# The value products of four attentions: one unit later in TensorE's order, low parts of the probabilities in a second sweep

## The chip, the cores and the metric

The kernel runs on one core of a Trainium2 chip. The metric is the device time of one execution in microseconds (us); the time before is the median of three runs.

## What is computed

Two blocks of a transformer on 512 tokens of width 1024, all in float32. The first block has a latent attention of 8 heads ("mla"), a short convolution, an attention of 4 heads over 256 memory rows ("mem"), gates and an output projection. The second has two causal attentions of 8 heads each, "fox" (with a bias from cumulated forget gates) and "dil" (windows of three dilations, folded into one mask), an output projection, and a layer of product-key experts. What the change touches is in each attention this:

```python
s = einsum('bqhd,bkhd->bhqk', q, k) * scale      # + bias, mask
p = softmax(s, axis=-1)
o = einsum('bhqk,bkhd->bqhd', p, v)
```

The experts come after all attentions, and take the second half of the time.

## The kernel before, in words

*Products in two parts.* TensorE works on rounded float32 (fp32r). Each operand x is split into a high part, hi (ScalarE copies x into the rounded type, L174 or L177 of `split`), and a low part, lo = x - hi (VectorE, L175 or L178). A product is then three matmuls into one PSUM tile, weights hi by data hi, hi by lo, lo by hi: L182, L183 and L184 of `mm`, or L194, L195 and L197 of `mtile`. In the trace these lines are the helper's; the tile tells which product it is: "mm" for scores, projections and gates (4 PSUM tiles), "tp" for transposes (2), "o" for value products (2).

*An attention in units.* `attention` (L321) cuts the work into units: one head h and one block i of 128 queries, so 16 units for mem, and 32 each for mla, fox and dil. nkc(i) is the number of chunks of 128 keys that block i looks at: 2 in mem, 4 in mla, i + 1 in fox and dil. The steps of a unit are: `s` scores (TensorE), `e` softmax without the division (VectorE and ScalarE, L308 to L315), `norm` division (VectorE L341 and L346, or ScalarE L344), `tr` transposes of the probabilities (TensorE, L354), `sp` split of the transposed probabilities from PSUM into a tile PT (ScalarE L174, VectorE L175), and `o` the value product (TensorE) with its evacuation. Two units, i even and odd, share one PT tile of 128 x 2 x 4 x 256 (hi and lo, key chunk, query), and `o` runs once for the pair, after the odd unit: for each key chunk three matmuls, vh by PT hi, vh by PT lo, vl by PT hi, over 256 queries, or over 128 for a chunk that only the odd unit looks at. So an `o` has 6 matmuls in mem, 12 in mla, and 6 or 12 in fox and dil. There are 8 + 16 + 16 + 16 = 56 of them.

*The order that is written.* Step j of `attention` writes out: scores of unit j; division and transposes of j - 1; softmax of j; split of j - 1; value product of j - 2. The attention has n + 2 such steps. Between steps, `merge` puts other tasks ("fills": gate, convolution, projection products) by their costs; mla's 34 steps of cost 2.0 share the fills in proportion, mem's first 14 steps and fox's and dil's first 32 have fills as well. `run` gives each task its weights, 4 loads ahead.

*The order that is run.* The whole program is handed to a scheduler at build time, which lists each engine's instructions: earlier written ones come first, but an instruction whose operands are not there yet, by the scheduler's own model of time, is passed by later ones that are ready. Engines then run their lists in order. SBUF tiles of the kind of PT (`b8`) come from a pool of NB8 = 16 buffers, and a new tile waits until an old one has had its last reader.

Of the kernel before, what the change touches and what calls it, by code (L numbers as in the profile page):

```python
# [25 lines left out]
              n1=8, n2=8, bfor=1, qh=96, kh=96, qhc=1, khc=1)  # L26
# [82 lines left out]
class Kernel:  # L109
# [211 lines left out]
    def attention(self, nh, nkc, scores, probs, v, evac, prep=None, cost=1.5, act=False):  # L321

        nc = self.nc
        units = [(h, i) for h in range(nh) for i in range(4)]
        st = {}

        def s(j):
            h, i = units[j]  # L330
            st["s", j] = self.psum("mm")
            scores(h, i, st["s", j])

        def e(j):
            h, i = units[j]
            st["P", j] = probs(h, i, st.pop(("s", j)))

        def norm(j):
            h, i = units[j]
            P, c = st["P", j]  # L340
            nc.vector.reciprocal(c[:, 3:4], c[:, 2:3])  # L341
            p = P[:, :nkc(i) * 128]
            if act:
                nc.scalar.activation(p, p, AF.Copy, scale=c[:, 3:4])  # L344
            else:
                nc.vector.tensor_scalar(p, p, c[:, 3:4], None, op0=ALU.mult)  # L346

        def tr(j):
            h, i = units[j]
            P, _ = st.pop(("P", j))  # L350
            n = nkc(i)
            tp = self.psum("tp")
            for kc in range(n):
                nc.tensor.transpose(tp[:, kc * 128:(kc + 1) * 128], P[:, kc * 128:(kc + 1) * 128],  # L354
                                    self.cst("ident"))
            st["t", j] = tp

        def sp(j):
            h, i = units[j]
            n = nkc(i)  # L360
            if i % 2 == 0:
                st["PT", h, i // 2] = self.b8(F32R, [128, 2, 4, 256])
            pt = st["PT", h, i // 2]
            q = (i % 2) * 128
            src = st.pop(("t", j))[:, :n * 128].rearrange("p (a b) -> p a b", a=n)
            self.split(pt[:, 0, :n, q:q + 128], pt[:, 1, :n, q:q + 128], src)

        def o(j):
            h, i = units[j]
            if i % 2 == 0:  # L370
                return
            pt = st.pop(("PT", h, i // 2))
            ps = self.psum("o")
            n0, n1 = nkc(i - 1), nkc(i)
            for kc in range(n1):
                c = slice(0, 256) if kc < n0 else slice(128, 256)
                vh, vl = v(h, kc)
                self.mm(ps[:, c], vh, vl, pt[:, 0, kc, c], pt[:, 1, kc, c], kc == 0, kc == n1 - 1)
            evac(h, i // 2, ps)

        tasks = []
        n = len(units)
        for j in range(n + 2):
            def step(j=j):
                if j < n:
                    h, i = units[j]
                    if prep is not None and i == 2 and h + 1 < nh:
                        prep(h + 1)
                    s(j)
                if 0 <= j - 1 < n:  # L390
                    norm(j - 1)
                    tr(j - 1)
                if j < n:
                    e(j)
                if 0 <= j - 1 < n:
                    sp(j - 1)
                if 0 <= j - 2 < n:
                    o(j - 2)
            tasks.append(Task(step, None, cost))
        return tasks  # L400

# [1429 lines left out]
```

## Time and profile before

| | us |
|---|---|
| median of three runs | 2168.97 (2168.51, 2168.97, 2172.50) |
| profiled execution | 2168.01 |
| its span on the core | 2166.3 |
| TensorE busy | 2113.3 |
| VectorE busy | 1652.2 |
| ScalarE busy | 976.5 |

The span is the time from the first to the last instruction of the program on the core. Busy time of TensorE is the union of its matmuls, whose ends are modelled; how fast they follow each other is seen from the differences of their starts. "Idle before" in brackets is the time in which the engine did nothing before an instruction, and behind the arrow stands the instruction whose end released it.

### The profile page before, as it was taken

What the parts mean: (1) busy time and instruction counts of PE and PEld (TensorE: products, weight loads), DVE (VectorE), ACT (ScalarE), POOL (GpSimd) and SP (SyncE); (2) the same over time, 40 slices, a digit from 0 to 9 for tenths busy, and PEclk for the clock granted to TensorE, in tenths of its full rate; (3) what the DMA queues carried; (4) which work ended last, traced back from release to release, by engine and by line L of the source; (5) the groups of instructions that cost most, each with busy time, mean ns of one, the idle gap of its engine ahead of it and who ended that gap; (6) DMA issues with size and microseconds to landing.
All of it is one profiled execution on the core that took longest, in us unless ns stands there. A gap on an engine that the chain in (4) does not pass through costs nothing. (4 is left out here: it accounts for less than half of the span.)

```text
span 2166.3 us, 30072 instructions
## 1 busy us (share of the span) xinstructions
PE 2113.3 (98%) x11091; PEld 1819.0 (84%) x11091; DVE 1652.2 (76%) x3491; ACT 976.5 (45%) x1493; POOL 486.1 (22%) x349
## 2 busy tenths in 40 slices
PE   8999999999999999999999899999999999999998
PEld 6787787888877888789999899999998888888786
DVE  6755565633457778799999999989859878877877
ACT  6454355623334555433344555566644333333332
POOL 0000000011200000100053454645544222222332
PEclk9999999999999999999999999999999999999999
DMA  6122211123323122222498898999999999999994
GB/s 226 57 87 69 88 59 49 59 88 136 93 86 110 47 60 78 62 76 78 157 356 295 296 342 316 348 338 340 343 326 348 331 340 353 331 344 345 325 345 160
DMA packets 159411, 448.86 MB, mean 207 GB/s; under 512 B 12952, under 2 KB 62872, under 8 KB 155552
## 3 DMA queue, kind: packets, MB, share of 16 engines
q1 hardware_dynamic: 114768, 265.26, 35.6%
q0 software_dynamic: 44352, 181.42, 22.6%
q8 instruction: 87, 1.43, 0.3%
q14 instruction: 60, 0.49, 0.1%
q10 hardware_dynamic: 144, 0.26, 0.0%
HBM read 397.59 MB, written 49.30 MB: 206 GB/s over the span
## 5 line engine op out<-in xcount | busy, mean ns | idle before, releaser
L174 ACT ACTIVATE whi<-wraw 128x1024 fp32r<-128x1024 f32 x388 | 408.8, 1054 | 685.9 <-PE mm L195 319.7
L175 DVE TENSOR_TENSOR wlo<-wraw,whi 128x1024 fp32r<-128x1024 f32 x388 | 471.1, 1215 | 186.5 <-ACT whi L174 125.6
L194 PE MATMUL mm<-b,whi 128*128 128x384 f32 (+1 forms) x1656 | 603.9, 366 | 8.2 <-ACT b L174 5.3
L195 PE MATMUL mm<-b,whi 128*128 128x384 f32 (+1 forms) x1656 | 596.2, 361 | 0.7 <-DVE b L175 0.7
L197 PE MATMUL mm<-b,wlo 128*128 128x384 f32 (+1 forms) x1656 | 369.0, 361 | 2.8 <-DVE wlo L175 2.8
L194 PEld LDWEIGHTS mm<-b,whi 128*128 128x128 f32 x1656 | 311.1, 188 | 39.8 <-ACT b L174 5.8
L195 PEld LDWEIGHTS mm<-b,whi 128*128 128x128 f32 x1656 | 311.2, 188 | 30.4 <-DVE b L175 2.5
L197 PEld LDWEIGHTS mm<-b,wlo 128*128 128x128 f32 x1656 | 297.5, 187 | 32.3 <-DVE wlo L175 3.4
L1662 PE MATMUL mm<-whi,b 128*128 128x512 f32 x1024 | 301.5, 394 | 0.0
L1521 POOL DMA_INDIRECT b<-in_peer_v,eidx x128 | 204.6, 1599 | 322.4 <-PE mm L1662 203.2
L1521 POOL DMA_INDIRECT b<-in_peer_un,eidx x128 | 194.7, 1521 | 256.1 <-PE mm L1662 88.2
L1662 PEld LDWEIGHTS mm<-whi,b 128*128 128x128 f32 x1024 | 192.3, 188 | 45.3
L1556 DVE SCALAR_TENSOR_TENSOR b<-b,gg,b 128x1024 f32<-128x1024 f32 x128 | 163.5, 1277 | 3.5 <-DMA b<-in_peer_v,eidx 3.4
L1550 DVE CUSTOM_DVE_ANT_0 b<-b,b 128x1024 f32<-128x1024 f32 x128 | 155.1, 1215 | 8.4 <-DMA b<-in_peer_un,eidx 8.4
L1662 PE MATMUL mm<-wlo,b 128*128 128x512 f32 x512 | 161.2, 394 | 0.0
L174 ACT ACTIVATE b<-b 128x384 fp32r<-128x384 f32 (+2 forms) x160 | 86.5, 546 | 164.2 <-DVE b L1630 125.1
L1662 PE MATMUL o<-whi,b 128*128 128x512 f32 x512 | 160.5, 394 | 0.0
L182 PE MATMUL mm<-b,whi 128*128 128x512 f32 x320 | 127.8, 399 | 2.9 <-ACT b L315 2.0
L184 PE MATMUL mm<-b,wlo 128*128 128x512 f32 x320 | 127.8, 399 | 0.0
L183 PE MATMUL mm<-b,whi 128*128 128x512 f32 x320 | 127.4, 398 | 0.0
L1662 PEld LDWEIGHTS mm<-wlo,b 128*128 128x128 f32 x512 | 96.2, 188 | 22.9
L1662 PEld LDWEIGHTS o<-whi,b 128*128 128x128 f32 x512 | 96.2, 188 | 22.6
(301 smaller groups left out, 3008.4 us busy)
## 6 DMA issues: line engine op xcount, KB each, us to landing
wraw<-in_peer_u SPq DMA_DIRECT2D x128, 512.0 KB, 6.2
wraw<-in_peer_v SPq DMA_DIRECT2D x128, 512.0 KB, 6.6
wraw<-in_w_in_ft SPq DMA_DIRECT2D x57, 512.0 KB, 3.4
gdram<-b POOLq DMA_DIRECT2D x24, 1024.0 KB, 9.3
b<-gdram SPq DMA_DIRECT2D x32, 768.0 KB, 12.9
hdram<-b POOLq DMA_DIRECT2D x28, 768.0 KB, 7.4
b<-hdram SPq DMA_DIRECT2D x28, 768.0 KB, 9.1
wraw<-in_w_out SPq DMA_DIRECT2D x16, 512.0 KB, 3.5
```

The costliest lines, as they stand in the source:

```text
L174: nc.scalar.activation(hi, x, AF.Copy)
L175: nc.vector.tensor_tensor(lo, x, hi.bitcast(F32), op=ALU.subtract)
L182: t.matmul(out, lhsT=wh, rhs=xh, start=start, stop=False)
L183: t.matmul(out, lhsT=wh, rhs=xl, start=False, stop=False)
L184: self.last = t.matmul(out, lhsT=wl, rhs=xh, start=False, stop=stop)
L194: t.matmul(ps[:M], lhsT=wh[:, k], rhs=xh(k), start=k == 0, stop=False)
L195: t.matmul(ps[:M], lhsT=wh[:, k], rhs=xl(k), start=False, stop=False)
L197: self.last = t.matmul(ps[:M], lhsT=wl[:, k], rhs=xh(k), start=False, stop=k == nk - 1)
L1521: d = nc.gpsimd.indirect_dma_start(out=t, out_offset=None, in_=a["peer_un" if kind == "u" else "peer_v"], in_offset=bass.IndirectOffsetOnA ...
L1550: nc.vector.tensor_tensor_reduce(t, t, st["xy"][:, 0], 1.0, 0.0, ALU.mult, ALU.add, st["hg"][:, s:s + 1])
L1556: nc.vector.scalar_tensor_tensor(st["xy"][:, 1], t, st["gg0"][:, s:s + 1], st["xy"][:, 1], op0=ALU.mult, op1=ALU.add)
L1662: K.last = nc.tensor.matmul(acc[2 * tt + j], lhsT=w[:, c], rhs=d, start=m == 0 and e == 0, stop=m == 127 and e == 2)
```

## The change

It touches `o` and the loop over steps in `attention`, and so all four attentions. In `o`, the three matmuls of a key chunk are no longer written together: a first sweep over the chunks writes vh by PT hi and vl by PT hi, a second sweep vh by PT lo. And step j writes the value product of unit j - 3 instead of j - 2; the attention has n + 3 steps. The steps before it are unchanged.

```diff
             n0, n1 = nkc(i - 1), nkc(i)
+
+            cols = lambda kc: slice(0, 256) if kc < n0 else slice(128, 256)
             for kc in range(n1):
-                c = slice(0, 256) if kc < n0 else slice(128, 256)
                 vh, vl = v(h, kc)
-                self.mm(ps[:, c], vh, vl, pt[:, 0, kc, c], pt[:, 1, kc, c], kc == 0, kc == n1 - 1)
+                nc.tensor.matmul(ps[:, cols(kc)], lhsT=vh, rhs=pt[:, 0, kc, cols(kc)], start=kc == 0, stop=False)
+                nc.tensor.matmul(ps[:, cols(kc)], lhsT=vl, rhs=pt[:, 0, kc, cols(kc)], start=False, stop=False)
+            for kc in range(n1):
+                self.last = nc.tensor.matmul(ps[:, cols(kc)], lhsT=v(h, kc)[0], rhs=pt[:, 1, kc, cols(kc)],
+                                             start=False, stop=kc == n1 - 1)
             evac(h, i // 2, ps)
 
         tasks = []
         n = len(units)
-        for j in range(n + 2):
+        LAG = 3
+        for j in range(n + LAG):
...
-                if 0 <= j - 2 < n:
-                    o(j - 2)
+                if 0 <= j - LAG < n:
+                    o(j - LAG)
```

## Rows read from the trace of the kernel before

**Rows 1.** The page: span, TensorE's busy time, and its granted clock by slices.

```profile
span 2166.3 us, 30072 instructions
...
PE 2113.3 (98%) x11091; PEld 1819.0 (84%) x11091; DVE 1652.2 (76%) x3491; ACT 976.5 (45%) x1493; POOL 486.1 (22%) x349
...
PEclk9999999999999999999999999999999999999999
```

**Rows 2.** Busy time of the engines in the four attention stretches.

```profile
core 0: us, PE busy (x) PEld busy (x) DVE busy (x) ACT busy (x) POOL busy (x), PEclk, DMA share, GB/s
130.00:185.00 55.00, 51.80 (x278) 43.40 (x278) 29.67 (x94) 32.41 (x79) 0.00 (x0) 1.00 0.18 60
265.00:440.00 175.00, 170.89 (x902) 141.55 (x901) 104.86 (x203) 100.16 (x177) 5.18 (x4) 1.00 0.17 58
680.00:785.00 105.00, 100.75 (x592) 84.60 (x592) 81.07 (x263) 57.40 (x144) 0.00 (x0) 1.00 0.18 56
785.00:880.00 95.00, 90.47 (x512) 76.28 (x510) 74.55 (x223) 49.82 (x120) 0.00 (x0) 1.00 0.17 56
sum 430.00, PE 413.91 PEld 345.84 DVE 290.15 ACT 239.78 POOL 5.18; mean PE 103.48 PEld 86.46 DVE 72.54 ACT 59.95 POOL 1.30
```

**Rows 3.** TensorE's waits, whole span: waiting, released by: total us, times, longest.

```profile
PE mm L464 <- ACT whi L177: 6.5, 2, 5.4
PE tp L1485 <- ACT b L1492: 6.2, 2, 5.5
...
PE mm L182 <- ACT b L315: 4.3, 10, 0.8
PE o L183 <- DVE b L175: 3.6, 7, 1.0
...
PE mm L182 <- DVE t L308: 2.1, 2, 1.2
PE o L182 <- ACT b L174: 1.4, 3, 0.7
...
PE tp L354 <- DVE b L178: 0.7, 1, 0.7
```

**Rows 4.** TensorE in order of time, fox: start, duration, instruction, idle before.

```profile
734.33 0.36 PE L182 MATMUL o<-b,b 128*128 128x256 f32 x1
734.62 0.50 PE L182 MATMUL mm<-b,b 128*128 128x128 f32 x2
736.14 0.38 PE L183 MATMUL o<-b,b 128*128 128x256 f32 x1 [1.02 <-DVE b L175]
736.37 0.28 PE L184 MATMUL o<-b,b 128*128 128x256 f32 x1
736.48 0.28 PE L182 MATMUL o<-b,b 128*128 128x256 f32 x1
736.60 0.28 PE L183 MATMUL o<-b,b 128*128 128x256 f32 x1
```

**Rows 5.** VectorE in the same stretch.

```profile
735.40 0.69 DVE L175 TENSOR_TENSOR b<-tp,b 128x512 fp32r<-128x512 f32 x1
```

**Rows 6.** TensorE in order of time, mem: two lone first matmuls.

```profile
147.41 0.29 PE L182 MATMUL o<-b,b 128*128 128x256 f32 x1
148.27 0.50 PE L182 MATMUL mm<-b,whi 128*128 128x512 f32 x1 [0.57 <-ACT b L315]
...
166.38 0.36 PE L182 MATMUL o<-b,b 128*128 128x256 f32 x1
167.31 0.39 PE L182 MATMUL mm<-b,b 128*128 128x256 f32 x1 [0.56 <-ACT b L315]
```

**Rows 7.** TensorE in order of time, end of dil.

```profile
867.46 0.28 PE L182 MATMUL o<-b,b 128*128 128x256 f32 x1
...
870.33 0.38 PE L182 MATMUL o<-b,b 128*128 128x256 f32 x1 [0.58 <-ACT b L174]
871.05 0.39 PE L183 MATMUL o<-b,b 128*128 128x256 f32 x1 [0.34 <-DVE b L175]
...
873.29 0.39 PE L182 MATMUL o<-b,b 128*128 128x256 f32 x1 [0.16 <-ACT b L174]
...
875.75 0.38 PE L182 MATMUL o<-b,b 128*128 128x256 f32 x1 [0.69 <-ACT b L174]
876.47 0.39 PE L183 MATMUL o<-b,b 128*128 128x256 f32 x1 [0.34 <-DVE b L175]
```

**Rows 8.** TensorE and, at 777.45, ScalarE in order of time, fox.

```profile
692.48 0.22 PE L182 MATMUL o<-b,b 128*128 128x128 f32 x1
692.53 0.27 PE L183 MATMUL o<-b,b 128*128 128x128 f32 x1
692.64 0.28 PE L184 MATMUL o<-b,b 128*128 128x128 f32 x1
...
776.85 0.28 PE L184 MATMUL o<-b,b 128*128 128x128 f32 x1
...
777.45 0.78 ACT L174 ACTIVATE b<-tp 128x256 fp32r<-128x256 f32 x2
...
777.86 0.38 PE L182 MATMUL o<-b,b 128*128 128x256 f32 x1
779.48 0.39 PE L182 MATMUL mm<-b,b 128*128 128x256 f32 x1 [1.23 <-DVE t L308]
...
784.72 0.27 PE L184 MATMUL o<-b,b 128*128 128x128 f32 x1
```

**Rows 9.** TensorE in order of time, mla.

```profile
333.34 0.39 PE L182 MATMUL o<-b,b 128*128 128x256 f32 x1
334.10 0.50 PE L182 MATMUL mm<-b,whi 128*128 128x512 f32 x1 [0.37 <-ACT b L315]
```

**Rows 10.** Value products by line, whole span; and weight loads of L183, by form.

```profile
L182 PE MATMUL o<-b,b x176: 220/282/388, 147.4 to 877.5; 128*128 128x256 f32 x144, 128*128 128x128 f32 x32
L183 PE MATMUL o<-b,b x176: 273/282/387, 152.8 to 877.6; 128*128 128x256 f32 x144, 128*128 128x128 f32 x32
L184 PE MATMUL o<-b,b x176: 273/281/364, 152.9 to 877.7; 128*128 128x256 f32 x144, 128*128 128x128 f32 x32
...
L183 PEld LDWEIGHTS o<-b,b 128*128 128x128 f32 x176 | 33.3, 189 | 6.8 <-DVE b L175 5.5
```

**Rows 11.** ScalarE's waits, 592 to 880 us.

```profile
ACT b L174 <- PE o L184: 32.2, 21, 3.1
```

## The prediction

> **What bounds the kernel now.** I read the page first: TensorE is busy 98% of the span, and its clock is at the higher of its two levels nearly everywhere [rows 1]. So a gain can only come from time in which TensorE stands still, or from fewer or cheaper matmuls; the change has as many matmuls as before. Then I read the stretches with attention in them [rows 2]: the memory attention (130 to 185 us), the latent attention (265 to 440), fox (680 to 785) and dil (785 to 880). TensorE is busy 413.9 of these 430 us, so 16.1 us of standing still is all that the attentions have. VectorE is busy 77 and 78% in the two causal stretches; it is behind at places, not bound.
>
> Then the waits of TensorE [rows 3]. Four of the groups belong to the attentions: the value products that wait for the low parts of the probabilities (3.6 us in 7 waits) and for the high parts (1.4 us in 3), and score or gate products on L182 that wait for ScalarE's exp to read its PSUM tile (4.3 us in 10) or for VectorE's L308 (2.1 us in 2). The two largest single waits of the page's list, at L464 and L1485, lie outside.
>
> Last the order itself. A value product (tile o) takes its first matmul, then stops: the next one needs the low parts, which VectorE subtracts after ScalarE's copy. In fox [rows 4] the first o matmul starts at 734.33, two score matmuls start behind it, and then TensorE stands still for 1.02 us until VectorE's subtraction, started at 735.40, is through [rows 5]. All 11 remaining o matmuls of that unit waited for this one subtraction, though the four products with the high parts on vh and the four on vl needed nothing but what the first matmul had. Of the 56 value products of the four attentions, 47 have such a lone first matmul, the first at 147.41 and the last at 867.46 [rows 6, 7].
>
> **The change part by part.** *(a) The waits of the value products themselves.* 3.6 + 1.4 = 5.0 us [rows 3]. One unit further back means that a whole unit of TensorE work lies between the split of the probabilities and their use. A unit in fox lasts (784.72 - 692.64) / 30 = 3.07 us, from the last matmul of fox's first value product to that of its sixteenth [rows 8]; the longest wait is 1.0 us [rows 3]. The cover is three times the longest wait, so away from the ends these waits go. At the end of dil nothing else is left to fill [rows 7]: there 0.58, 0.34, 0.16, 0.69 and 0.34 us, 2.1 of the 5.0, are spent. After the change the value product of unit 29 (six matmuls, 0.7 us) moves behind the last transposes, and the last one starts its eight high-part products (8 x 0.12 = 0.94 us, the spacing of [rows 4]) when ScalarE is done. That covers the 0.34 us for the low parts and 0.5 of the 0.69 us. I keep 0.5 us there and take 4.5 us of gain; the bounds are 2.9 us (the tail keeps all) and 5.0.
>
> *(b) Starting up again.* The matmul that ended a wait has its successor 0.23 us later (736.14 to 736.37), a running one 0.12 us later [rows 4]. Ten waits by 0.11 us is 1.1 us; I take 1.0 (bounds 0 and 1.1).
>
> *(c) Stalls right behind a lone o matmul.* TensorE, with nothing else ready in the order that was written out, goes on to a score or gate product whose PSUM tile is not yet free: 0.93 us from start to start at 166.38 and 0.86 at 147.41 [rows 6], 0.76 at 333.34 and three times more at other heads [rows 9], 1.62 at 777.86 [rows 8]. Less the 0.12 us that the matmul takes, the seven sum to 0.93 + 0.86 + 4 x 0.76 + 1.62 - 7 x 0.12 = 5.6 us. A value product whose operands are all there has 6 or 12 matmuls (0.7 or 1.4 us) to put in that place, more than each stall but one. Whether it stands there depends on the order that the scheduler draws up, and some of the products will already have been used up earlier. Bounds 0 and 5.6; the rows show neither end as nearer, I take half, 2.8.
>
> *(d) Lone matmuls.* Most cost nothing: the next instruction starts 0.12 us later. A dozen have it 0.20 us later; 12 x 0.08 = 1.0 us, of which I take 0.5 (bounds 0 and 1.0).
>
> *(e) The second sweep.* Before, vh was used twice in a row and then vl; after, vh, vl, and vh again later. The instruction count is the same: 176 + 176 + 176 matmuls [rows 10]. Each of them has a weight load of its own: the 176 products with low parts have 176 loads of 189 ns, though the matmul before had the same weights [rows 10]. So I put the second sweep at zero. The Trainium skill, "TensorE: Matmul & The Clock Gate", Part 2, says that weights typically stay put and can be loaded once for several matmuls; by that the change would lose 176 reuses. The trace has no such reuse here to lose. In fox and dil the last chunk is 128 columns wide: of its three matmuls the second comes 0.06 us after the first, the third 0.11 us after that [rows 8]. After the change the third stands alone behind a 256-column one; by these two spacings that is at most 32 x 0.05 = 1.6 us either way. I take zero.
>
> *(f) What runs on.* Each attention has one more step at its end. In the latent attention the fills are spread over 35 steps instead of 34, so the end still has cover; fox runs straight into dil; the memory attention's end runs into gate products. Only dil's end is bare, counted in (a). No DMA is added or removed, and VectorE's, ScalarE's and GpSimd's own work is the same; what reads tile o (the evacuations on ScalarE or VectorE) comes with it one unit later in their queues. Nothing is put ahead of SyncE's weight loads but by the shift of the fills.
>
> The sum: 4.5 + 1.0 + 2.8 + 0.5 = 8.8 us. TensorE that doesn't stop at one place comes sooner to the next that waits for the same late engine; VectorE has over a fifth of its time free [rows 2] and can make most of that up, so I give back 0.8 us and take 8.0. The profiled execution took 2168.0 us (span 2166.3 and 1.7 around it), so it would be 2160.0. The median of the three runs is 1.0 us above it: 2161.
>
> **The rivals.** *The wait only moves.* If VectorE's lateness is what counts, TensorE waits as long at the next transpose or score. For it: the score products already wait 2.1 us for L308. Against it: the transposes of L354, which close the chain of the softmax, have one wait of 0.7 us in the whole list [rows 3]. It would leave the time at 2165 to 2171.
>
> *Everything near tile o goes.* All of (a) to (d) at the upper bound is 5.0 + 1.1 + 5.6 + 1.0 = 12.7 us: 2156 on the scale of the median, and with some of the stalls between score products 2152.
>
> *The probability tiles run out (slower).* They come from a pool of 16 buffers, and in fox 14 are taken (normed input 4, residual 2, forget rows 2, values 4, output 2), so two are left. The split of unit 2p+4 has to wait until value product p has read its tile. In fox that split already follows closely: the last o matmul of unit 27 starts at 776.85 and ScalarE's splits at 777.45 [rows 8], a margin of 0.6 us less the matmul's own time, while ScalarE waits for the end of value products for 32.2 us in 21 waits [rows 11]. If the product now comes a unit (3.07 us) later than the transposes of that split, the margin turns into some 1.5 to 2.5 us of delay, and both PSUM tiles for transposes stay full. Sixteen pairs by 1.5 us is 24 us if no projection fills it, 12 us if half is filled; less the 8 us of gain that gives 2173 to 2185, and I take 2179. It decides at one point: whether a ready value product is put ahead of the transposes two units on. In the order as written it is, and nothing that it reads is late any more; that speaks against it.
>
> *The lost reuse of weights*, by the rule named in (e): 176 loads of 0.19 us that were not there before is 33 us, 2202. The rows have the loads already.
>
> **How the numbers follow.** The forecast (2156 to 2164.5, likeliest 2161) has 0.48; everything near tile o goes (2152 to 2156) 0.12; the wait only moves (2165 to 2171) 0.24; the tiles run out 0.14; lost reuse 0.02. A different order may also shift stalls in the later stages, which I count in the width of each. The range that leaves out no more than two in ten goes from 2151 to 2173. What a measurement can tell from no change is about 0.2%, 4.3 us: faster, under 2164.6, 0.60; within, 0.26; slower, 0.14.
>
> **What the profile after would show.** Right: the rows for o matmuls waiting for L174 and L175 are gone but for the last one in dil; value products stand in unbroken runs of 6 or 12; TensorE's idle time in the four stretches falls from 16 us to about 10. Wrong: the same microseconds beside waits of transposes or scores (the wait moved), or ScalarE's splits waiting longer for value products and TensorE's transposes behind them (the tiles ran out). Wrong in the sum: lone first matmuls remain although the operands are there, because the scheduler still breaks the products up.

## The result and the profile after

The changed kernel takes 2154.6 us (median of six runs, 2152.8 to 2155.0) against 2168.7 us (2167.7 to 2172.5): the ratio is 0.9932, with a 95% interval of 0.9922 to 0.9942. That is 14.2 us less; 8 were forecast. It is faster and inside the range, but below the forecast's own bracket (2156 to 2164.5) and where the rival "everything near tile o goes" had put it (2152 to 2156).

The page of after [rows 1]:

```profile
span 2153.2 us, 30081 instructions
...
PE 2107.9 (98%) x11091; PEld 1819.7 (85%) x11091; DVE 1651.9 (77%) x3491; ACT 977.0 (45%) x1493; POOL 467.9 (22%) x349
```

The span fell by 13.1 us. TensorE has the same 11091 matmuls, yet its busy time fell by 5.4 us (2113.3 to 2107.9). So only 7.7 us of the 13.1 were time that the trace shows as standing still; the other 5.4 us had been booked as work. That is where the sum was too small.

The busy times of the four stretches [rows 2], same windows:

```profile
130.00:185.00 55.00, 52.72 (x281) 43.94 (x280) 29.59 (x96) 33.28 (x83) 0.00 (x0) 1.00 0.20 68
265.00:440.00 175.00, 171.16 (x908) 143.06 (x907) 104.16 (x204) 100.22 (x178) 5.17 (x4) 1.00 0.17 58
680.00:785.00 105.00, 103.68 (x620) 87.95 (x619) 87.45 (x274) 59.93 (x149) 0.00 (x0) 1.00 0.18 56
785.00:880.00 95.00, 93.90 (x526) 80.53 (x525) 76.19 (x214) 54.73 (x123) 3.94 (x3) 1.00 0.19 62
```

TensorE stands still for 8.5 us there instead of 16.1, and it is in fox (1.3 for 4.3) and dil (1.1 for 4.5) that it stopped less. In fox 620 matmuls fall into the 105 us, where 592 did. (The last window holds more than dil now, whose last value product starts at 866.8.)

TensorE's waits, whole span [rows 3]:

```profile
PE tp L1491 <- ACT b L1498: 6.3, 3, 4.9
...
PE mm L182 <- ACT b L177: 4.1, 5, 1.6
PE o L379 <- ACT b L174: 2.4, 3, 1.1
PE mm L182 <- ACT b L315: 1.6, 4, 0.8
...
PE mm L182 <- DVE t L308: 0.9, 1, 0.9
```

L379 and L380 are the first sweep (vh, vl by PT hi), L382 the second (vh by PT lo); lines further down are six higher than before, L1485 is L1491. No value product waits for low parts any more (3.6 us in 7 before). Waiting for the high parts went up, from 1.4 to 2.4 us in 3. Score products wait less for L315 (4.3 to 1.6) and L308 (2.1 to 0.9), those on L177 more (4.1).

TensorE in fox, the place of [rows 4] (start, duration, instruction):

```profile
734.41 0.50 PE L354 MATMUL tp<-c_all,b 128*128 128x128 f32 x3
734.67 0.36 PE L379 MATMUL o<-b,b 128*128 128x256 f32 x1
734.87 0.28 PE L380 MATMUL o<-b,b 128*128 128x256 f32 x1
734.99 0.22 PE L379 MATMUL o<-b,b 128*128 128x128 f32 x1
735.05 0.28 PE L380 MATMUL o<-b,b 128*128 128x128 f32 x1
735.16 0.62 PE L354 MATMUL tp<-c_all,b 128*128 128x128 f32 x4
735.54 0.42 PE L382 MATMUL o<-b,b 128*128 128x256 f32 x2
735.80 0.44 PE L182 MATMUL mm<-b,b 128*128 128x128 f32 x2
```

A value product now starts with all its high-part matmuls, transposes of another unit stand between its two sweeps, and no bracket is left.

*Where the 13.1 us went.* I cut both traces at four instructions, into five stretches. From the start to mem's last value product: 193.6 and 193.4 us. From there to fox's first: 497.4 and 496.2 (mla lies in it). From there to dil's last: 186.7 and 177.1. From there to the first product of the experts: 131.3 and 129.0. The rest: 1157.3 and 1157.4. So 9.6 + 2.3 us of it are fox and dil with their tail, and 1.3 us all the rest of the attentions. Below, "C" is the third of these, fox's first to dil's last value product: 186.7 before, 177.1 after. In C TensorE stands still for 7.0 us before and 1.0 after.

### The profile page after: what moved, and what is told of

Read it like the earlier page. It is cut to its first block, busy times and chain, and to the rows that moved or that the text cites. A ratio compares the mean times of both kernels' runs of the same rounds, so it can differ in the third digit from the quotient of the medians.

```text
span 2153.2 us, 30081 instructions
## 1 busy us (share of the span) xinstructions
PE 2107.9 (98%) x11091; PEld 1819.7 (85%) x11091; DVE 1651.9 (77%) x3491; ACT 977.0 (45%) x1493; POOL 467.9 (22%) x349
## 4 chain that ended last, share of the span: by engine, by line
PE 90%; DVE 8%; ACT 1%; issue 0%; DMA 0%; SPq 0%; DVEq 0%; ACTq 0%
PE mm L1668 17%; PE mm L194 14%; PE mm L197 14%; PE mm L195 13%; PE o L1668 8%; PE mm L182 6%; PE mm L183 5%; PE mm L184 5%; PE tp L1491 2%; PE tp L354 1%; DVE wlo L175 1%; PE o L379 1%; PE o L380 1%; PE o L382 1%; DVE b L1304 1%; DVE tk L1302 1%
## 5 line engine op out<-in xcount | busy, mean ns | idle before, releaser
L1527 POOL DMA_INDIRECT b<-in_peer_v,eidx x128 | 198.1, 1548 | 334.2 <-PE mm L1668 203.7
L1527 POOL DMA_INDIRECT b<-in_peer_un,eidx x128 | 183.1, 1430 | 255.0 <-PE mm L197 90.0
L183 PE MATMUL mm<-b,whi 128*128 128x512 f32 x320 | 127.4, 398 | 0.0
```

The source lines that it names most:

```text
L183: t.matmul(out, lhsT=wh, rhs=xl, start=False, stop=False)
L1527: d = nc.gpsimd.indirect_dma_start(out=t, out_offset=None, in_=a["peer_un" if kind == "u" else "peer_v"], in_offset=bass.IndirectOffsetOnA ...
```

## What held ScalarE: a loop that the traces don't bear out

[Rows 11] stood in the prediction only as evidence on buffers. They suggest a mechanism of their own, which has to be checked. ScalarE in fox, before (start, duration, instruction, idle before):

```profile
732.96 0.38 ACT L174 ACTIVATE b<-o 64x256 fp32r<-64x256 f32 x1
733.36 0.60 ACT L174 ACTIVATE b<-tp 128x512 fp32r<-128x512 f32 x1
...
737.68 0.38 ACT L174 ACTIVATE b<-o 64x256 fp32r<-64x256 f32 x1 [2.19 <-PE o L184]
738.09 0.39 ACT L174 ACTIVATE b<-tp 128x256 fp32r<-128x256 f32 x1
```

and VectorE in the same place:

```profile
733.08 0.69 DVE L1086 TENSOR_TENSOR b<-mm,b 128x512 f32<-128x512 f32 x1 [1.64 <-PE mm L184]
733.69 1.22 DVE L175 TENSOR_TENSOR wlo<-wraw,whi 128x1024 fp32r<-128x1024 f32 x1
734.94 0.43 DVE L175 TENSOR_TENSOR b<-o,b 64x256 fp32r<-64x256 f32 x1
```

The evacuation (b<-o) is a split too: ScalarE copies tile o, VectorE subtracts. At 737.68 ScalarE had stood for 2.19 us at the evacuation of one value product, and the split of the next probabilities (b<-tp, 738.09) is behind it in the same queue. That looks like a loop: a late product holds ScalarE, which would split the next probabilities late, which would make the next product late. ScalarE's waits in 592 to 880 us, beside [rows 11]; before:

```profile
ACT b L174 <- PE tp L354: 14.8, 15, 3.0
```

and after:

```profile
ACT b L174 <- PE tp L354: 37.6, 36, 2.5
ACT b L174 <- PE o L382: 4.9, 3, 1.8
```

The waits for value products fell from 32.2 us in 21 to 4.9 in 3. ScalarE stands about as long as before, but now for transposes.

The starts of the splits speak against the loop. The transposes that the split of 738.09 reads stand right behind the late product in TensorE's own order:

```profile
737.49 0.40 PE L354 MATMUL tp<-c_all,b 128*128 128x128 f32 x2
```

They end at 737.89, so the split came 0.2 us after its input and not 2.19. In fox and dil 29 of the 64 splits stand right behind an evacuation that had waited; they start 0.15 us in the median (1.10 at most, 6.9 in all) after the end of their last transpose. Over all 64 units ScalarE's split starts 0.24 us in the mean behind the transposes before and 0.14 after, and VectorE's subtraction 0.80 behind that split before and 0.68 after. So the two engines deliver hardly any earlier after the change; the products ask later, as the prediction had it.

What made the subtraction of 735.40 late [rows 5], for which the product of 736.14 waited 1.02 us [rows 4], stands ahead of it in VectorE's queue: L1086, which had itself waited 1.64 us for a projection, the split of a weight tile (1.22 us), and the evacuation. Of the 1.44 us between the end of ScalarE's copy (733.36 + 0.60) and the subtraction the evacuation is 0.43.

## The experiments

Each ran beside the kernel before, which took 2167.9 to 2168.8 us in these batches; a ratio is to that. Two readings stood against each other first: that the second sweep is what covers the low parts, or that the step further back is.

**One half of the change each.** The second sweep alone, against the kernel after:

```diff
-        LAG = 3
+        LAG = 2
```

> Undoes the second part of the change: the value product of unit j - 2 in step j, as before; the low parts stay in a second sweep. Theory A (the sweep covers the wait: eight or four products with the high parts, 0.94 or 0.47 us, stand where one stood while VectorE subtracts): 2155 to 2158, TensorE idle in fox and dil near 1 to 2 us in place of 7.0. Theory B (the distance of one unit covers it): 2161 to 2166, idle in fox and dil 4 to 6 us. Theory C (any new order shifts a few stalls): anything from 2157 to 2168, with no idle time that follows the sweep.

Measured: 2156.8 us, 0.9947 (0.9931 to 0.9964), C 183.2 us.

The step back alone, the sweep undone:

```diff
-                nc.tensor.matmul(ps[:, cols(kc)], lhsT=vh, rhs=pt[:, 0, kc, cols(kc)], start=kc == 0, stop=False)
...
+                self.mm(ps[:, c], vh, vl, pt[:, 0, kc, c], pt[:, 1, kc, c], kc == 0, kc == n1 - 1)
```

> Undoes the first part: the three matmuls of a key chunk together again (vh hi, vh lo, vl hi), the value product one unit further back as in the changed kernel. Theory A: 2165 to 2169, lone first matmuls and their waits stay, idle in fox and dil 5 to 7 us. Theory B: 2155 to 2158, waits of value products for the low parts gone. Theory C: 2157 to 2168.

Measured: 2159.7 us, 0.9960 (0.9946 to 0.9974), C 178.1 us. By the totals the sweep alone is the faster of the two, and its 2156.8 us is what theory A had named; but 7.4 us between their profiled runs lie in the experts, where both have the same instructions (1152.8 and 1160.1 us; more on that at the end of the next part). C, where the change is, ranks them the other way: the step back gives 8.6 of the 9.6 us, the sweep 3.5, and together they give 9.6, so they remove in part the same. TensorE's waits in 592 to 890 us say why; of the sweep alone:

```profile
PE o L379 <- ACT b L174: 2.8, 5, 0.7
PE o L382 <- DVE b L175: 2.0, 3, 1.1
```

and of the step alone:

```profile
PE o L183 <- DVE b L175: 0.9, 2, 0.6
...
PE o L182 <- ACT b L174: 0.3, 2, 0.2
```

The value products waited for 5.2 us before. With the sweep alone they still wait 4.8, more of it now for the high parts; with the step alone 1.3. TensorE's idle time in C is 5.0 us with the sweep alone, where theory A had 1 to 2 and theory B 4 to 6, and 1.3 with the step alone, where theory A had 5 to 7. So theory B has the waits right and the totals wrong. ScalarE's waits for value products, 29.6 us with the sweep alone and 7.9 with the step alone, fall in the same order; that they are not the cause is seen below, with the low parts taken out of the wait.

**One step further, and one empty step.** Both halves with the value product two units further back, against the kernel after; and the kernel before with only an empty step at the end of each attention, which spreads mla's fills over 35 steps:

```diff
-        LAG = 3
+        LAG = 4
```
```diff
-        for j in range(n + 2):
+        for j in range(n + 3):
```

> Both parts, with one unit more: the value product of unit j - 4 in step j. Theory A: 2153 to 2156, as the changed kernel, since the cover is the sweep. Theory B: 2151 to 2154, a little better again. If the two free buffers for probability tiles decide anything, this is slower: over 2158, with splits that wait for value products.

> Neither part: the kernel before with one empty step at the end of each attention, so that only the spread of the fills over 35 steps in the latent attention is left of the change. Theories A and B: 2167 to 2170, no change. Theory C: a shift of 2 to 8 us either way.

Measured: 2152.0 us, 0.9927 (0.9911 to 0.9944), C 176.8 us for the first; 2169.4 us, 1.0004 (0.9995 to 1.0014), C 186.8 for the second. Two units back is not told apart from one by the total, and C says that nothing is left to gain: TensorE stands still in it for 0.9 us, for 1.0 in the kernel after. The rival with the probability tiles falls here too, since a tile is held for one unit more and C is no longer. The empty step moves nothing that can be measured in the total; in its profiled run the stretch from mem to fox is 3.3 us longer than before (500.7 us).

**Which attentions.** Both halves in fox and dil only, and in mem and mla only:

```diff
-    fox = K.attention(8, nkc, fox_scores, fox_probs, v_of("fv"), evac("fox"), act=ACTS[0])
+    fox = K.attention(8, nkc, fox_scores, fox_probs, v_of("fv"), evac("fox"), act=ACTS[0], lag=3, sweep=True)
...
```

> Both parts of the change in fox and dil alone; the memory and the latent attention as before. The traces so far put 9.6 us of the gain into fox and dil, 1.0 us into the stretch behind dil, and next to nothing into the two early attentions (memory 1.6 less, with 1.7 more ahead of it; latent 1.3 less). Theory (the gain sits where VectorE is busiest): 2156 to 2159. Rival (each attention has its share, as the prediction's terms (a) and (c) had it): 2161 to 2164.

> Both parts in the memory and the latent attention alone; fox and dil as before. Theory: 2165 to 2169. Rival: 2160 to 2164.

Measured: 2158.2 us, 0.9958 (0.9944 to 0.9972), C 177.1; and 2166.7 us, 0.9994 (0.9984 to 1.0003), C 186.7. C is as in the kernel after, to 0.1 us, in the first and as before in the second. In mem and mla the change is not told apart from none.

**The spread of the fills undone.** The kernel after, with mla's last step at next to no cost, so that its fills stand as before; the same with two units back:

```diff
-            tasks.append(Task(step, None, cost))
+            tasks.append(Task(step, None, cost if spread or j < n + 2 else 1e-6))
```

> The changed kernel, but the latent attention's last step has no weight in the spread of the fills, so that they lie as in the kernel before. The empty step alone cost 3.0 us of idle or late starts in the latent attention, by its trace. Theory (the spread of the fills costs the change what the sweep gains there): 2150 to 2152.5. Rival (the loss was one of that order alone): 2153 to 2157.

> Both parts with unit j - 4 in step j, and the fills of the latent attention spread as before the change: the two variants that came out lowest, together. If their gains add: 2149 to 2151. If both are one and the same room in the latent attention, or differences of single builds: 2151 to 2154.

Measured: 2152.3 us, 0.9928 (0.9911 to 0.9945), C 177.1; and 2157.6 us, 0.9953 (0.9936 to 0.9970), C 176.9. Each of the two seemed worth 2 us by itself (2152.0 and 2152.3), and both together came out 3 us slower than the kernel after. C is the same in all, and what differs lies outside it. In the profiled runs the experts take 1157.4 us in after, 1153.0 with two units back, 1158.8 with the spread undone and 1160.3 with both; with the spread undone fox's first value product comes 4.0 us earlier than in after (685.7 for 689.7), and that is its gain. The two gains don't add, and 2157.6 lies above both ranges of the expectation.

**The low parts taken out of the wait.** The kernel before, its low-part products reading the high parts:

```diff
-                self.mm(ps[:, c], vh, vl, pt[:, 0, kc, c], pt[:, 1, kc, c], kc == 0, kc == n1 - 1)
+                self.mm(ps[:, c], vh, vl, pt[:, 0, kc, c], pt[:, 0, kc, c], kc == 0, kc == n1 - 1)
```

> The kernel before with its old order (three matmuls of a chunk together, unit j - 2 in step j), where the product with the low parts reads the high parts instead: no value product waits for VectorE's subtraction, which still runs. The low parts of the probabilities are left out of the result. Theory A (the wait for the low parts is what the change removes): 2154 to 2158. Theory B (the distance also removes waits for ScalarE's copy, 2.1 us or more at the end of dil and ahead of scores): 2159 to 2163.

Measured: 2153.0 us, 0.9932 (0.9915 to 0.9948), C 179.8. Taking away the waits for low parts alone gives 6.9 of the 9.6 us of C, where the list has 3.6 us for them in 7 waits [rows 3] (with the 0.3 us a wait that is found below, 5.8). TensorE's idle time in C is 3.0 us, nearly all of it waits for high parts. The low part of the total is again the experts' (1155.1). The order that is run changed along with it, since the scheduler had no late operand to pass: 2 products start with a lone first matmul, for 47. ScalarE's waits for value products in 592 to 880 us:

```profile
ACT b L174 <- PE o L184: 24.2, 22, 3.0
```

ScalarE is held three quarters as long as before, and most of C's gain is there all the same. So C follows what TensorE's products wait for, and not how long ScalarE is held.

**Twice the subtraction.** In fox and dil VectorE subtracts every low part twice, in the kernel before and in the kernel after:

```diff
+            if not act:
+                nc.vector.tensor_tensor(pt[:, 1, :n, q:q + 128], src, pt[:, 0, :n, q:q + 128].bitcast(F32), op=ALU.subtract)
```

> The kernel before, with VectorE's subtraction of the low parts done twice in fox and dil (64 more subtractions of 0.28 to 0.69 us, some 31 us of VectorE, which has 44 us free in the two stretches). Theory (a low part that comes later is paid by TensorE where the distance is short): 8 to 20 us over the kernel before, 2176 to 2188. Rival (VectorE's throughput is what counts): 15 to 30 us here and the same number in the changed kernel.

> The changed kernel with the same doubled subtraction in fox and dil. Theory: 1 to 6 us over the changed kernel, 2155 to 2161, less than half of what the kernel before pays. Rival: as much as the kernel before pays, 2170 to 2185.

Measured: 2197.0 us, 1.0136 (1.0119 to 1.0153), and 2182.8 us, 1.0071 (1.0055 to 1.0088): 29 and 28 us more than the same kernel without it. I had expected the changed order to hide it and it doesn't; the rival was right. VectorE is not out of time for it: it is busy for 80.3 of 105 us in fox and 83.2 of 95 in dil in the kernel after with it, 77 and 78% before [rows 2]. What changes is who waits. TensorE's waits, in the kernel before with it (the second subtraction is L368):

```profile
PE o L183 <- DVE b L368: 9.5, 9, 1.6
```

and in the kernel after with it (L384 is the second sweep):

```profile
PE tp L354 <- DVE b L368: 7.6, 8, 2.7
...
PE o L384 <- DVE b L368: 2.4, 2, 1.6
```

The value products wait 2.4 us for low parts instead of 9.5, and the transposes 7.6 us where there was no such wait: their PSUM tile is free only when the subtraction has read it. That is the rival "the wait only moves", at a VectorE that comes later still. The change buys cover, and no earlier subtraction. Which chain makes up all of the 28 us was not isolated.

**The evacuation taken out of the queue's way.** The kernel before; in fox and dil the evacuation reads the value tile instead of tile o, so that ScalarE and VectorE do the same work without waiting for a product:

```diff
-            K.split(st[nm, "ohi"][rr, h // 2, c], st[nm, "olo"][rr, h // 2, c], ps[rr, :256])
+            K.split(st[nm, "ohi"][rr, h // 2, c], st[nm, "olo"][rr, h // 2, c], st[nm[0] + "v", "hi"][rr, 0, :256].bitcast(F32))
```

> The kernel before (old order, one unit less between), but in fox and dil ScalarE's copy of an attention's value product out of tile o, and VectorE's subtraction behind it, read 64 x 256 elements of the value tile in SBUF instead of tile o: both engines do the same number of instructions of the same size, and neither stands in its queue waiting for a value product. What is left out: the value products of fox and dil are computed but not read, so the output differs. Theory Q (ScalarE, held in its queue by the copy that waits for the product before, splits the next probabilities late, and that is most of what the change removes): ScalarE's 32.2 us of waits for value products in 592 to 880 us go to under 5, the time from fox's first value product to dil's last goes from 186.7 to 177 to 181 us (the change has 177.1), the whole to 2153 to 2161. Theory P (the value product itself stands too close behind its split, whatever ScalarE was doing): ScalarE's waits go but that time stays at 184 to 187 us, and the whole at 2163 to 2168.

Measured: 2164.5 us, 0.9981 (0.9971 to 0.9990). ScalarE's waits for value products are gone, as theory Q had asked, but the total is theory P's: 4.3 us less, of the 14.2. The copies didn't stay where they were, though. ScalarE in order of time:

```profile
692.25 5.20 ACT L174 ACTIVATE b<-b 64x256 fp32r<-64x256 f32 x14
697.96 0.72 ACT L174 ACTIVATE b<-b 64x256 fp32r<-64x256 f32 x2
787.87 5.62 ACT L174 ACTIVATE b<-b 64x256 fp32r<-64x256 f32 x15
```

and TensorE's waits in 592 to 890 us:

```profile
PE mm L182 <- DVE t L308: 2.2, 3, 1.1
PE mm L194 <- DVE t L308: 2.2, 1, 2.2
...
PE o L182 <- ACT b L174: 1.5, 3, 0.7
```

Ready at once, all 16 copies of fox ran in one heap at 692 to 699 us, and those of dil at 788 to 794. The new waits stand around these heaps, 2.2 us in 701 to 707 and 3.6 in 790 to 820, and TensorE's granted clock was 0.87 in 700 to 710 us and 0.96 in 710 to 720, after it had stood still for 2.2 us in the first of these; before, it was 1.00 in both. C can't be read either: other tasks slid in ahead of dil's last product (C 202.5 and the tail 111.1 us, 313.6 together; before 318.0, after 306.1). What can be read is the stretch away from the heaps. From 707 to 788 us TensorE waits not once; before it waited there five times, 1.02 [rows 4], 0.41, 0.31, 1.23 [rows 8] and 0.28 us, 3.3 in all. But more than the hold is gone from it. The evacuation's subtractions of 0.4 us are gone too, three of which stood right ahead of a subtraction that TensorE waited for (VectorE is busy for 57.2 us in the stretch, 60.4 before), and TensorE ran part of it at the lower clock. So this run doesn't isolate the loop through ScalarE, and the starts of the splits and the run without the low-part wait speak against it as the main cause. What the evacuation costs by its place in VectorE's queue stays open.

## Why the prediction was right, and where its sum was too small

*(a) The products' own waits: right in fox and dil, with less cover than was reckoned.* All of the 5.0 us of [rows 3] lie there, in ten waits and an eleventh of 0.1 us, 5.2 us together. After, 0.6 us is left, in two: 4.6 gained, 4.5 forecast, and the tail of dil has the 0.51 us that I kept (the forecast had 0.5):

```profile
865.41 0.38 PE L379 MATMUL o<-b,b 128*128 128x256 f32 x1 [0.51 <-ACT b L174]
...
866.40 0.63 PE L382 MATMUL o<-b,b 128*128 128x256 f32 x4
867.50 1.20 PE L194 MATMUL mm<-b,whi 128*128 128x512 f32 x4 [0.47 <-ACT b L174]
```

What I did not see coming are two new waits for high parts in mem and mla, 0.75 and 1.10 us. They are the rest of the 2.4 us in the list. And the cover is not "a whole unit of TensorE work", 3.07 us. The matmuls that stand in the list between a unit's last transpose and its first low-part product are, at their usual spacing, 4.24 us in the median of fox before and 5.66 after, in dil 3.68 and 4.65: 1.4 and 1.0 us more. The scheduler had already moved the products back; the written step is not the distance that runs. In dil the smallest distance was 0.12 us and became 1.16. Between the end of the split and the low-part product the traces of fox and dil have 1.57 us in the median before (10 of 32 under 0.15) and 3.06 after (1 of 32). Most of that is the added cover; the splits themselves are 0.2 us earlier in the mean. That the distance is the cause, and not a faster split, is shown by the step alone (C 178.1) and by the run without the low-part wait (C 179.8).

*(b) Starting up again: the term that was mis-sized.* I took 0.11 us a wait, from the successor, 1.0 us in all. The idle in brackets begins at the modelled end of the matmul before, which is 0.23 to 0.39 us after its start in these waits, while a running TensorE starts the next one 0.12 us after. From start to start the eleven waits cost 7.5 us over the usual spacing, with 5.2 us of recorded idle: 0.21 us a wait were booked as work ahead of the bracket, and 0.105 behind it. That is 2.3 + 1.2 = 3.5 us before, 0.4 after: 3.1 gained, three times the term. It is the larger part of what the page shows as 5.4 us less busy time for the same matmuls.

*(c) Stalls behind a lone matmul.* In fox I counted half of one stall; the whole of it went, 1.5 us and 0.1 behind it, from [rows 8]. In mem and mla the waits for L315 fell from 4.3 to 1.6 us, but those for L177 rose from 2.8 to 4.1 us and the two new waits of (a) came: from the start to fox's first product only 1.3 us is gained, of some 2.3 that (c) and (d) had there, and the run with mem and mla alone isn't told from no change.

*Not in the sum.* Two waits beside tile o that I had read as outside: a score product at 788.94 (0.55 us, for L1169) and the projection behind dil at 880.34 (0.69 us, for the low part of the last evacuation). The second is gone, 0.96 us with what lies around its bracket. The first is still there in the kernel after, with 0.39 us at 782.14, and 0.26 us cheaper from start to start. Together that is 1.2 us.

*(e) The second sweep* was put at zero with 1.6 us either way. The 128-column low-part matmul alone behind a 256-column one is followed after 0.07 us in the mean, where the third of three was after 0.11: by all spacings inside a product some 1.1 us for the 32 products of fox and dil, a gain inside the bound. The loads are as they were: after, the 176 low-part matmuls that come back to vh have 176 loads of 190 ns, as the 176 had before [rows 10]. By what the Trainium skill says of weights that stay put ("TensorE: Matmul & The Clock Gate", Part 2) a reuse could have been lost; neither trace has one. After:

```profile
L382 PEld LDWEIGHTS o<-b,b x176: 186/190/193, 154.3 to 866.7; 128*128 128x128 f32 x176
L382 PE MATMUL o<-b,b x176: 220/282/373, 154.5 to 866.8; 128*128 128x256 f32 x144, 128*128 128x128 f32 x32
```

*The sum again*, for fox, dil and the tail: 4.6 + 3.1 + 1.6 + 1.2 + 1.1 = 11.6 us, against 11.9 measured between the marks (9.6 + 2.3); the forecast had some 6.5 there. With 1.3 us gained before fox and 0.2 given back in the experts that is 12.7, for 13.1 us of span. The 0.8 us that I gave back is not seen: VectorE is 83% busy in fox, for 77% [rows 2], and no new wait for it in fox and dil stands in the list.

*The signs that were named.* Idle time in the four stretches: about 10 forecast, 8.5 measured. The o rows: gone but for dil's last, plus two in mem and mla. Unbroken runs of 6 or 12: wrong. The products stand in 110 pieces where there were 106; they break between the sweeps, and only the lone first matmuls went, from 47 to 3. It cost nothing, since each piece is now ready when its turn comes. With the step back alone there are still 53 lone first matmuls, and C is 178.1; with the sweep alone there is none, and C is 183.2. Being alone was never the cost, and (d), put at 0.5 us, has nothing to show.

*The rivals.* "Everything near o goes" was right on the time, in part by luck: (b) came out at nearly three times its upper bound, and (c) at no more than half of its own. "The wait only moves" is wrong here (no transpose of the attentions stands in the list of waits after), and is seen with VectorE doubled. "The tiles run out" is wrong: ScalarE's waits for value products went down, and one more unit cost nothing. "Lost reuse" is wrong by the loads.

*The experts' stage* takes 1152.8 to 1160.3 us in these builds with the same instructions. Much of that is one wait of transposes for the stage's own evacuations, and the clock behind it. In the two builds with the shortest stage, the sweep alone and two units back, the wait is 1.5 and 1.2 us long; in the kernel before and the kernel after it is 5.5 and 4.9, with the step alone 4.8, with the spread undone 6.0. Busy time of TensorE, its weight loads, VectorE, ScalarE and GpSimd, and the granted clock, around that wait; in the kernel after and with the sweep alone:

```profile
1190.00:1204.00 14.00, 9.12 (x54) 8.70 (x53) 13.97 (x18) 5.69 (x8) 3.11 (x3) 0.76 0.53 197
1190.00:1204.00 14.00, 12.81 (x95) 12.28 (x94) 13.93 (x27) 7.29 (x11) 5.79 (x5) 1.00 0.97 366
```

In the kernel after the clock fell to the lower of its two levels within the wait (1192.4 to 1197.3) and came back at 1201.2; with the sweep alone it stayed at 1.00. By an estimate the 3.9 us at half the clock cost 2.0, and the wait is 3.4 longer: 5.4 us, for the 4.6 us between these two builds. Why the wait differs from build to build is open. It moves totals by as much as half of this change, so the parts of the change were compared by C and not by totals.

## What to carry to other kernels

Where an engine waits for another one's late result, one step of distance in the written order can take away the waits although the late engine is no faster. Before a long wait in a producer's queue is called the cause, look when the instruction behind it had its own inputs: ScalarE stood for 32.2 us, and the splits behind it were late by a median of 0.15. Size a wait from start to start, not by its bracket: here each cost 0.3 us more than its recorded idle. To compare variants that differ by a few us, cut the traces at instructions that all of them have, so that scatter of a later stage stays out.

## What the runs showed of the hardware

A 128-column matmul behind a 256-column one is followed after 0.07 us, one behind another 128-column one after 0.11: the order of widths is worth some 1 us here. With VectorE's subtractions doubled, TensorE's granted clock fell: to a mean of 0.95 in fox for the kernel after (680 to 785 us, of which TensorE stood still for 10.1) and of 0.96 in dil for the kernel before (785 to 880, 8.6 still), where both kernels without that work have 1.00; part of these stretches was run at the lower of the two levels, 1.2 instead of 2.4 GHz. So of the 28 us at most some 5 (0.05 x 105, an estimate) are lost clock and not waiting.
